# One cast held behind a copy in the forgetting stages, and four stores moved behind eight transpositions: a hybrid attention block

## The chip, the cores and the metric

The kernel runs on one core of a Trainium2 chip. The metric is the device time of one execution in microseconds (us), and lower is better. A core has TensorE (PE, with its weight loads shown apart as PEld), VectorE (DVE), ScalarE (ACT), GpSimd (POOL) and SyncE (SP), which in this kernel issues all DMA transfers. Each engine works through its own instruction queue in order; semaphores order the engines among each other.

## What is computed

The reference is one decoder block with two attention branches over 16 meta tokens and 512 real ones. Cut to what matters here:

```python
u = rmsnorm(h, pre_norm_g)
cq, ckv, k_pe_raw, z_mla, fq, fk, fv, f_logit, z_fox, gate_a, gate_b = split(u @ w_in)
# latent branch, 16 heads: low-rank q, k, v, and 32 rotary dimensions
q = rmsnorm(cq) @ w_uq ; kv = rmsnorm(ckv) @ w_ukv
q_m = concat(q_nope, rope(q_pe)) ; k_m = concat(k_nope, rope(k_pe_raw) for all heads)
y_mla = (causal_attention(q_m, k_m, v_mla) * silu(z_mla)) @ w_br_mla
# forgetting branch, 16 heads: logits get cum[t] - cum[s]
cum = cumsum(log_sigmoid(f_logit + fox_forget_b))
y_fox = (causal_attention(fq, fk, fv, cum) * silu(z_fox)) @ w_br_fox
mixed = (sigmoid(gate_a) * y_mla + sigmoid(gate_b) * y_fox) @ w_out
h = h + rmsnorm(mixed, post_norm_g)
```

All is float32 with a width of 1024.

## The kernel before

Every large product is computed from a high and a low part of each operand: of three products two use the weights' high part, one the low part. Weights come in units of 128 output columns: SP loads the raw weights (`wraw`, 512 KB, three buffers), ACT casts them to the high part (`wh`, line 127, three buffers), POOL subtracts to get the low part (`wl`, line 102), and then PE works. The raw buffer is free again when POOL is done, `wh` when PE is done with the unit. Loads are asked for three units ahead.

The attention runs in 16 stages, one for each pair of heads of each branch, in turn: even stages are forgetting ones (`br` = 1), odd ones latent (`br` = 0). `si` is the stage, from 0; `pr` the pair. A stage is, on PE:

- scores of the first three query blocks (`s0`: blocks of 144, 272 and 400 columns), then the values of the stage before (`va`, line 801, tile `ov`), then the scores of the fourth block (`s1`);
- the list `fill`: projections that this and the next stage need. A forgetting stage fills with the forgetting z unit (8 steps), the next latent q (2 steps), the latent z (its first step is `fill[11]`), latent k and v. A latent stage fills with the next forgetting q, the first half of k, v, and the second half of k. A step's first call casts the weights of its unit.

In between, at places set by hand, come `n0` and `n1` (line 767): they scale the exponentials to probabilities in two float16 parts (`pn`) and issue eight DMA transpositions (`pt`), which the values of that stage need, in the next one. `fill[0]` issues the transposition of the stage's value vectors (`vp`).

The copies of projected K and Q out of PSUM (`hlk`, `hlq`, line 239 on ACT, then DVE for the low part) are recorded in `halved`, one entry for each half of K. The exponentials are line 763, DVE's score reductions line 755.

Rotary queries of the latent branch are computed for eight heads at a time (`pe_unit`). Those of the first two heads go to their place (`QP`) directly; those of the other six of the first group are stored to DRAM by `store0(x, 2, 8)`, two stores for each of two x, 192 KB each (`qpe_dram<-gT`), and read back one pair at a time, 256 KB with both halves, by `load_qp` (`QP<-qpe_dram`), for the first time for stage 3. The second group, all eight heads, is stored in stages 6 and 7 behind `n1`.

PE's order is the order in the program. The other queues are ordered by a planner that works with its own estimates of when things are ready. Two means bind it: `tc.issue_after(x)` puts what is traced in its block behind x on x's engine, without a wait for x to end; `keep_in_program_order` puts an instruction behind the one that was traced before it on its engine. Casts are issued behind `behind[0]` while that list has an entry:

```python
with tc.issue_after(behind[0]) if behind else nullcontext():
    nc.scalar.copy(wh[:, :n], raw[:, :n])
```

and every DMA that is traced while `written[0]` is true is kept in program order on SP.

Of the kernel before, what the change touches and what calls it, by code (L numbers as in the profile page):

```python
# [54 lines left out]
def block_kernel(ctx: ExitStack, tc: tile.TileContext, x, meta_tokens, pre_norm_g, w_in, fox_forget_b,  # L55
# [28 lines left out]
    written, sums_out = [False], []  # L84
    behind, through, first_t, exps, halved = [], [], [], [], {}
# [126 lines left out]
    def run(steps):  # L212
        for _, fn in steps:
            fn()
# [309 lines left out]
    def gate_unit():  # L524

        i, br = gates.pop(0)

        def done(_, ps):
            ths[i, br] = thp.tile([128, S], F32, tag="th", name=f"th{i}{br}")
            nc.scalar.activation(ths[i, br], ps, AF.Tanh, scale=0.5)  # L530
        return unit(f"pg{i}{br}", win_w((O_GA, O_GB)[br], i), u_act, KD, REAL, done)


    with ExitStack() as att:
# [289 lines left out]
        def feed(br, pr):  # L824

            q = (q_mla, q_fox)[br](pr)
            k = (k_mla, k_fox)[br](pr)
            v, vts[br, pr] = v_unit(br, pr)
            return q, k, v
# [7 lines left out]
        pe, rest0, store0 = pe_unit(0)  # L837
# [5 lines left out]
        for si, (br, pr) in enumerate(stages):  # L843
            last = si + 1 == len(stages)
            if not last:
                q, k, v = feed(*stages[si + 1])
            if br == 1:

                za, zb = z_unit(1, pr), z_unit(0, pr)
                fill = (vts[br, pr] if pr else begun) + za + q + zb[:4] + k + zb[4:6] + v + zb[6:]  # L850
            elif not last:

                fill = vts[br, pr] + q + k[:KD] + v + k[KD:]
            else:
                g = gate_unit()
                fill = vts[br, pr] + g + gate_unit() + gate_unit()
# [9 lines left out]
        for si, (br, pr) in enumerate(stages):  # L866
            s0, s1, n0, n1, va = attention(br, pr)

            for fn in [s0] + late + [s1]:
                fn()  # L870

            fill = fills[si]
            if si == 0:

                run(fill[:5])
                run(vts[1, 0] + pe_rest)
                n0()
                n1()
                first_t.extend(through)
                run(fill[5:])  # L880
            else:
                run(fill[:1])
                if si == 1:

                    written[0] = True
                    for x in range(2):
                        store0(x, 2, 8)
                    written[0] = False
                run(fill[1:5])
                if si == 1:  # L890

                    behind[:] = exps[:1]
                if si == 2:
                    behind.clear()
                n0()
                run(fill[5:12])
                n1()
                if 6 <= si < 8:

                    written[0] = True  # L900
                    rest1(si - 6)
                    written[0] = False
                run(fill[12:])
            written[0] = False
            if si == 1:

                behind[:] = [halved[("k", 1, 1), 0]]
            late = [va]
# [146 lines left out]
```

## Time and profile before

| | us |
|---|---|
| median of 3 runs | 625.7 |
| lowest and highest | 625.54, 627.62 |
| span of the profiled execution, first to last instruction | 622.1 |
| PE busy in it | 599.9 (96%) |
| ACT busy | 330.8 (53%) |
| DVE busy | 315.4 (51%) |
| POOL busy | 265.5 (43%) |

Of the profiled execution only the span is on record; what lies around it is taken as the difference to the median, 3.6 us. PE's busy time is of pipelined matmuls whose ends are modelled, so PE can be late where it is counted as busy. Times of single events below are counted from the start of the span. Stage 0 has its first scores at about 66.8 us, stage 15 its last at about 401; behind the stages come the gates, the branch outputs and the output projection, which PE runs through without a break.

### The profile page before, as it was taken

What the parts mean: (1) busy time and instruction counts of PE and PEld (TensorE: products, weight loads), DVE (VectorE), ACT (ScalarE), POOL (GpSimd) and SP (SyncE); (2) the same over time, 40 slices, a digit from 0 to 9 for tenths busy, and PEclk for the clock granted to TensorE, in tenths of its full rate; (3) what the DMA queues carried; (4) which work ended last, traced back from release to release, by engine and by line L of the source; (5) the groups of instructions that cost most, each with busy time, mean ns of one, the idle gap of its engine ahead of it and who ended that gap; (6) DMA issues with size and microseconds to landing.
All of it is one profiled execution on the core that took longest, in us unless ns stands there. A gap on an engine that the chain in (4) does not pass through costs nothing.

```text
span 622.1 us, 11008 instructions
## 1 busy us (share of the span) xinstructions
PE 599.9 (96%) x3811; PEld 507.3 (82%) x3811; DVE 315.4 (51%) x922; ACT 330.8 (53%) x757; POOL 265.5 (43%) x270
## 2 busy tenths in 40 slices
PE   5997999799999999999999999999999999999996
PEld 5886789689889789888888898887888888888885
DVE  3848647555765764674675657627321122024034
ACT  7755745655764864774676657656322222232321
POOL 4307535352346543344443523542744444444610
PEclk9999999899999999999999999999999999999999
DMA  9422589969798787878579697871433332333602
GB/s 289 99 76 53 120 178 142 242 141 190 145 186 161 149 208 154 172 167 204 140 161 174 145 169 159 187 168 40 136 102 101 102 93 79 100 103 115 257 34 102
DMA packets 223512, 89.31 MB, mean 144 GB/s; under 512 B 141708, under 2 KB 216852, under 8 KB 223456
## 3 DMA queue, kind: packets, MB, share of 16 engines
q1 hardware_dynamic: 223456, 88.61, 61.9%
q8 instruction: 30, 0.49, 0.3%
q14 instruction: 26, 0.21, 0.1%
HBM read 54.43 MB, written 4.00 MB: 94 GB/s over the span
## 4 chain that ended last, share of the span: by engine, by line
PE 86%; DVE 5%; ACT 4%; issue 2%; DMA 1%; SPq 0%; POOL 0%; DVEq 0%; ACTq 0%
PE z L96 14%; PE pg L96 14%; PE py L96 14%; PE v L96 9%; PE fq L96 7%; PE po L96 7%; PE fk L96 7%; PE st L96 5%; PE ov L96 3%; PE psm L96 3%; DVE sf L755 2%; PE mq L96 2%; ACT wh L127 2%; PE mk L96 1%; DVE vh L690 1%
## 5 line engine op out<-in xcount | busy, mean ns | idle before, releaser
L102 POOL TENSOR_TENSOR wl<-wraw,wh 128x1024 fp32r<-128x1024 f32 (+1 forms) x90 | 207.3, 2308 | 221.0 <-ACT wh L127 219.2
L127 ACT CAST wh<-wraw 128x1024 fp32r<-128x1024 f32 (+1 forms) x90 | 89.9, 1003 | 172.3 <-issue 47.7
L763 ACT ACTIVATE sf<-sf,nb 128x144 f32<-128x144 f32 (+3 forms) x128 | 72.0, 564 | 15.8 <-DVE nb L755 15.8
L791 DVE SCALAR_TENSOR_TENSOR pn<-sf,ri,pn 128x128 f16<-128x128 f32 (+3 forms) x128 | 68.8, 576 | 13.1 <-ACT pn L790 12.2
L790 ACT ACTIVATE pn<-sf,ri 128x128 f16<-128x128 f32 (+3 forms) x128 | 61.5, 551 | 19.9 <-ACT sf L763 17.9
L938 DVE SCALAR_TENSOR_TENSOR tb<-th,py 128x512 f32<-128x512 f32 x16 | 11.0, 687 | 101.9 <-PE py L96 101.9
L96 PE MATMUL st<-hlk,hlq 64*128 64x272 f32 (+3 forms) x480 | 52.8, 317 | 5.0 <-ACT hlk L239 4.1
L96 PE MATMUL z<-uTh,wh 128*128 128x512 f32 x128 | 50.8, 397 | 0.0
L96 PE MATMUL pg<-uTh,wh 128*128 128x512 f32 x128 | 50.2, 392 | 0.0
L96 PE MATMUL z<-uTh,wl 128*128 128x512 f32 x128 | 50.1, 391 | 0.0
L96 PE MATMUL z<-uTl,wh 128*128 128x512 f32 x128 | 49.9, 390 | 0.0
L96 PE MATMUL pg<-uTh,wl 128*128 128x512 f32 x128 | 49.8, 389 | 0.0
L96 PE MATMUL pg<-uTl,wh 128*128 128x512 f32 x128 | 49.8, 389 | 0.0
L96 PE MATMUL py<-gh,wh 128*128 128x512 f32 x128 | 49.8, 389 | 0.0
L96 PE MATMUL py<-gl,wh 128*128 128x512 f32 x128 | 49.8, 389 | 0.0
L96 PE MATMUL py<-gh,wl 128*128 128x512 f32 x128 | 49.8, 389 | 0.0
L96 PEld LDWEIGHTS st<-hlk,hlq 64*128 64x128 f32 x480 | 37.0, 186 | 15.0 <-ACT hlk L239 5.8
L755 DVE CUSTOM_DVE_ANT_0 sf<-st,maskt 128x272 f32<-128x272 f32 (+2 forms) x128 | 48.4, 434 | 0.9 <-PE st L96 0.8
L777 POOL TENSOR_TENSOR mt<-sf,ri 128x96 f32<-128x96 f32 (+1 forms) x32 | 9.5, 297 | 89.4 <-DVE ri L772 66.5
L96 PE MATMUL v<-uTh,wh 128*128 128x256 f32 (+1 forms) x128 | 36.6, 286 | 2.3 <-DVE hlk L102 2.3
L96 PE MATMUL v<-uTl,wh 128*128 128x256 f32 (+1 forms) x128 | 36.5, 285 | 0.0
L96 PE MATMUL fk<-uTl,wh 128*128 128x256 f32 (+1 forms) x128 | 36.4, 285 | 0.0
(189 smaller groups left out, 1403.3 us busy)
## 6 DMA issues: line engine op xcount, KB each, us to landing
wraw<-in_w_in_dram SPq DMA_DIRECT2D x56, 512.0 KB
wraw<-in_w_br_fox_dram SPq DMA_DIRECT2D x8, 512.0 KB
wraw<-in_w_br_mla_dram SPq DMA_DIRECT2D x8, 512.0 KB
wraw<-in_w_out_dram SPq DMA_DIRECT2D x8, 512.0 KB
pt<-pn SPq DMA_TRANSPOSE x128
xr<-in_x_dram SPq DMA_DIRECT2D x4, 512.0 KB
out_dram<-yo SPq DMA_DIRECT2D x8, 256.0 KB
QP<-qpe_dram SPq DMA_DIRECT2D x7, 256.0 KB
```

The lines of the kernel that those rows point to most:

```text
L96: nc.tensor.matmul(*a, **k)
L102: eng.tensor_tensor(out=lo, in0=src, in1=f32(hi), op=ALU.subtract)
L127: nc.scalar.copy(wh[:, :n], raw[:, :n])
L690: nc.vector.scalar_tensor_tensor(out=lo, in0=p, scalar=sc[:, 3:4], in1=hi, op0=ALU.mult, op1=ALU.subtract)
L755: nc.vector.tensor_tensor_reduce(out=sf_of(h, b)[:, c0 : c0 + w], in0=ps[h][:, o : o + w], in1=maskt[:, m0 : m0 + w], scale=-scale, scalar ...
L763: exps[g] = nc.scalar.activation(sf, sf, AF.Exp, bias=sums["nb"][:, h, b : b + 1], scale=-1.0, accum_out=sums["su"][:, h, b : b + 1]).ins
L777: nc.gpsimd.tensor_tensor(out=mt, in0=src, in1=ri.unsqueeze(3).broadcast_to([128, 2, nb_, META]), op=ALU.mult)
L790: nc.scalar.activation(hi, sf, AF.Copy, scale=rib)
L791: nc.vector.scalar_tensor_tensor(out=lo, in0=sf, scalar=rib, in1=hi, op0=ALU.mult, op1=ALU.subtract)
L938: nc.vector.scalar_tensor_tensor(out=tb[br], in0=ths[i, br], scalar=1.0, in1=py, op0=ALU.add, op1=ALU.mult)
```

## The change

Two edits in the stage loop, for all stages but the first.

1. In forgetting stages (`br` = 1, from stage 2 on), the list `behind` holds the copy of the second half of this stage's K while `fill[11]` runs, so that the cast of the first latent z unit's weights is issued behind that copy on ACT. In stage 2 such a hold already stands for an earlier cast, that of the forgetting z unit, behind the copy of the first half.
2. In stage 1, the four stores of the rotary queries of heads 2 to 7 are traced behind `n1` instead of behind `fill[0]`. As they are kept in program order, they stand on SP behind the last of that stage's eight transpositions, and no longer behind the transposition of the value vectors.

```diff
             else:
                 run(fill[:1])
+                run(fill[1:5])
+                if si == 1:
+                    behind[:] = exps[:1]
+                if si == 2:
+                    behind.clear()
+                n0()
+                run(fill[5:11])
+                if br:
+                    behind[:] = [halved[("k", 1, pr), 1]]
+                run(fill[11:12])
+                if br:
+                    behind.clear()
+                n1()
                 if si == 1:
                     written[0] = True
                     for x in range(2):
                         store0(x, 2, 8)
                     written[0] = False
-                run(fill[1:5])
-                if si == 1:
-                    behind[:] = exps[:1]
-                if si == 2:
-                    behind.clear()
-                n0()
-                run(fill[5:12])
-                n1()
                 if 6 <= si < 8:
```

No instruction is added or removed.

More of the change, by code (lines that the diff above doesn't have):

```diff
@@ L882, in block_kernel @@
                 run(fill[:1])
-                if si == 1:
[L885 to L888, printed above, removed]
                 run(fill[1:5])
@@ L895, in block_kernel @@
                 n0()
-                run(fill[5:12])
-                n1()
+                run(fill[5:11])
[4 more added lines that the diff above has]
+                    behind.clear()
+                n1()
+                if si == 1:
+                    written[0] = True
+                    for x in range(2):
+                        store0(x, 2, 8)
+                    written[0] = False
                 if 6 <= si < 8:
```

## The prediction

> **What bounds the kernel now.** I read the page first, for the chain that ended last, then that chain in order of time, then each engine around the two places where the chain leaves PE, then SP's queue.
>
> ```profile
> span 622.1 us, 11008 instructions
> PE 86%; DVE 5%; ACT 4%; issue 2%; DMA 1%; SPq 0%; POOL 0%; DVEq 0%; ACTq 0%
> ```
>
> PE carries the chain, so time can only be won where PE stands still. The chain, in order of time (start, length, what):
>
> ```profile
> 109.63 4.28 DMA wraw<-in_w_in_dram
> 113.99 1.04 ACT wh L127
> ...
> 116.97 2.93 PE ov L96 x26
> ...
> 121.07 5.66 PE z L96 x24
> ...
> 158.46 1.05 ACT wh L127
> ...
> 164.06 5.68 PE z L96 x24
> ...
> 375.78 1.05 ACT wh L127
> ```
>
> Twice a pattern shows. In stage 2 (the second forgetting stage) the chain runs through a weight load, then a cast of weights on ACT. In the six later forgetting stages (first 158.46, last 375.78) a cast of 1.05 us stands in the chain just ahead of the scores. The cast is that of the first latent z unit: it takes the buffer that the K unit frees with its last matmul, and the copy of the second half of K waits for the same matmul. Around it in stage 4, all engines in order of time:
>
> ```profile
> 159.39 0.30 PE L96 MATMUL st<-CT,ONE 64*128 64x272 f32 x2
> 159.41 0.36 ACT L239 CAST hlk<-fk 128x256 fp32r<-128x256 f32 x1
> 159.83 0.30 PEld L96 LDWEIGHTS st<-hlk,hlq 64*128 64x128 f32 x4 [0.36 <-ACT hlk L239]
> 160.15 0.30 DVE L755 CUSTOM_DVE_ANT_0 sf<-st,maskt 128x144 f32<-128x144 f32 x1
> 160.49 0.42 ACT L763 ACTIVATE sf<-sf,nb 128x144 f32<-128x144 f32 x1 [0.71 <-DVE nb L755]
> 160.85 2.04 PE L96 MATMUL ov<-pt,vp 80*64 80x512 f16 x26
> ```
>
> The 1.05 us is not PE's loss. Scores of the first two query blocks need only the first half of K and run until 159.69; only the 400-column block waits for the copy. The same place in a latent stage, where nothing waits, gives the price (PE alone):
>
> ```profile
> 179.17 0.29 PE L96 MATMUL st<-KPL,QP 64*128 64x272 f32 x2
> ...
> 179.84 0.34 PE L96 MATMUL st<-KPH,QP 64*128 64x400 f32 x2
> 180.02 0.35 PE L96 MATMUL st<-KPL,QP 64*128 64x400 f32 x2
> 180.29 0.41 PE L96 MATMUL ov<-pt,vp 80*64 80x512 f16 x2
> ```
>
> From the last 272-column pair to the values' first matmul it takes 1.12 us with five sets of 400 columns; one set is 0.18, so four take 0.94. The forgetting stage takes 160.85 - 159.39 = 1.46. It loses 0.52.
>
> **The cast order, stages 4 to 14.** The change issues that cast behind the copy. The copy then starts when the cast did, 158.46, and ends at 158.82; the cast ends at 159.87. The loss of 0.52 goes: 6 x 0.52 = 3.1 us. The lower bound is the wait that the row names, 0.36, so 2.2. What is late next? DVE's first reduction can start when PE's block ends, 159.69 instead of 160.15, so the first exponential comes 0.46 earlier, at 160.03, still after the cast's 159.87. The transpositions of the probabilities follow the exponentials and move with them, so their lead before the next stage's values stays nearly what it was. The cast's remainder on POOL ends 0.4 later; who waits for that is a rival below.
>
> **Stage 2: cast order and stores together.** PE alone:
>
> ```profile
> 111.74 0.30 PE L96 MATMUL st<-CT,ONE 64*128 64x272 f32 x2
> 115.36 1.28 PE L96 MATMUL st<-hlk,hlq 64*128 64x400 f32 x6 [3.31 <-ACT hlk L239]
> ```
>
> By starts, from the last 272-column pair to z: 121.07 - 111.74 = 9.33 us here, 164.06 - 159.39 = 4.67 in stage 4, and there 0.52 is lost as well. So 9.33 - 4.67 + 0.52 = 5.2 us are lost in stage 2. Not all of it is idle time. Behind the gap PE runs at half speed for a while (stretches of the span; the last three columns are the granted clock, the DMA engines' busy share and GB/s):
>
> ```profile
> 94.00:98.00 4.00, 4.00 (x20) 3.26 (x19) 3.95 (x8) 3.81 (x8) 3.74 (x6) 1.00 0.39 120
> 115.30:117.00 1.70, 1.64 (x10) 1.14 (x12) 1.60 (x9) 0.99 (x6) 1.70 (x1) 0.55 1.07 265
> ```
>
> The first row is for the stores: DMA engines busy 0.39, 120 GB/s, while SP is past them. SP's queue around stage 1, and around stage 7, where two stores of the second group already stand behind the transpositions; between them the start of the values in stage 9 on PE stands last:
>
> ```profile
> 91.63 4.07 SPq L90 DMA_DIRECT2D qpe_dram<-gT  x4
> ...
> 110.33 3.74 SPq L90 DMA_TRANSPOSE pt<-pn  x2
> ...
> 121.19 1.18 SPq L90 DMA_TRANSPOSE pt<-pn  x1
> ...
> 124.71 8.58 SPq L90 DMA_TRANSPOSE pt<-pn  x6
> ...
> 231.80 10.65 SPq L90 DMA_TRANSPOSE pt<-pn  x8
> 242.50 1.24 SPq L90 DMA_DIRECT2D qpe_dram<-gT  x2
> ...
> 249.76 0.35 SPq L90 DMA_DIRECT2D QP<-qpe_dram  x1
> ...
> 257.57 9.38 SPq L90 DMA_TRANSPOSE pt<-pn  x6
> ```
> ```profile
> 268.63 0.41 PE L96 MATMUL ov<-pt,vp 80*64 80x512 f16 x2
> ```
>
> The cast order by itself would win little in stage 2. The values there need all eight transpositions of stage 1, the last of which SP issued until 110.33 + 3.74 = 114.07. The shortest way from the end of such an issue to the values is in stage 8: 268.63 - (257.57 + 9.38) = 1.68. So the values, now at 116.97, could not start before 115.75.
>
> Moving the stores gives the rest. Four issues (4.07 us on SP) leave the place ahead of every load and transposition of stage 1. The last transposition then ends at 110.0 or sooner; without the stores' data in front, the last two would take 2 x 1.33 (10.65 for eight in stage 7) and not 3.74, so 108.9 to 110.0. Add 1.68: 110.6 to 111.7. PE's values are due at 111.74 + 0.94 = 112.68, so they don't wait. The z unit's weights (issued 109.63, landed 4.28 later) come by 105.6 + 4.28 = 109.9. The cast's turn is later: it starts 0.93 ahead of the 272-column row in stage 4, here at 110.8, and 0.36 of copy come before it, 111.2. Stage 2 gains its whole 5.2; if the transpositions came no earlier at all, 1.2 by the values' bound above.
>
> **Where the moved stores cost.** Behind the last transposition stand the stores, then whatever SP issues next: weight loads, the next values' transposition, the reload of QP for stage 3, and the eight transpositions of stage 2. The reload reads what the stores write, so SP stands still at it until they have landed. Two rows show that this happens:
>
> ```profile
> SPq L90 <- DMA qpe_dram<-gT: 4.3, 1, 4.3
> ```
> ```profile
> qpe_dram<-gT SPq DMA_DIRECT2D x4, 256.0 KB
> qpe_dram<-gT SPq DMA_DIRECT2D x4, 192.0 KB
> ```
>
> In stage 7, two stores of 256 KB held the reload for 249.76 - 242.50 = 7.3 us after the first issue. Here it is four of 192 KB. At the 120 GB/s of the row above, the extra 256 KB take 2.1 us: 9.4. Doubling the whole wait gives 14.5. I take 10.0, near the low end, because part of the 7.3 is the transposition ahead.
>
> So the reload is free at 109.4 + 10.0 = 119.4, the first transposition of stage 2 goes at 119.9, the eight take 12.1 (121.19 to 133.29), and 1.68 later, at 133.6, the values of stage 3 may start. They are due 180.29 - 160.85 = 19.4 after those of stage 2: 132.1. I charge 1.5 us. The ends: nothing (reload placed behind the transpositions, or landed sooner), and 5.6 to 6.7 with 14.5 us.
>
> By the Trainium skill (DMA: Bandwidth & Descriptors, "Why a DMA increments its semaphore by 16 and not by 1", the part on how many engines) a DMA uses the largest number up to 16 that divides the slowest dimension of both sides. Six heads would give six engines, and 6/16 = 0.375 agrees with the 0.39; eight heads would give eight, and estimated by that page four stores take 3.2 us longer than two rather than 2.1: the charge would be about 2 us and the time 619.4. It speaks against the change: the stores are slow wherever they stand.
>
> The sum, against the profiled execution (span 622.1; the median of 625.7 lies 3.6 above it, and I keep that difference): -3.1 - 5.2 + 1.5 = -6.8, a span of 615.3 and a time of **618.9 us**.
>
> For the charge in stage 3 I count idle time alone. By rows, a gap of 3.31 was followed by a clock of 0.55; if a gap of 1.5 were followed by a shorter such stretch in proportion, 0.9 us would be added. By the Trainium skill (TensorE: Matmul & The Clock Gate, "What's actually happening") the clock halves after an idle window of about 3.4 us, and by that rule 1.5 us of idle adds nothing; the 3.31 with the 0.55 behind it agrees roughly.
>
> **Rivals.** *The reload never binds* (it is placed late, or the stores land in under 9 us): 617.4. For it, SP has work to issue meanwhile; against it, the one row of 4.3 us is just this wait. Chance 0.27, the forecast 0.40.
>
> *The reload takes back stage 2* (14.5 us): 617.4 + 5.6 to 6.7 = 623.0 to 624.1, no measurable change against half a per cent of 625.7, which is 3.1 us and about what can be told here. For it: two stores alone stopped SP for 4.3. Against: weight loads, too, stood in that wait. Chance 0.15.
>
> *The held cast goes too late, slower.* If the order puts the cast behind the six exponentials and not right behind the copy, its remainder on POOL frees the raw weights later, and SP's next loads stand ahead of the transpositions:
>
> ```profile
> L763 ACT ACTIVATE sf<-sf,nb 128x144 f32<-128x144 f32 (+3 forms) x128 | 72.0, 564 | 15.8 <-DVE nb L755 15.8
> ```
> ```profile
> 159.59 2.38 POOL L102 TENSOR_TENSOR wl<-wraw,wh 128x1024 fp32r<-128x1024 f32 x1 [1.80 <-ACT wh L127]
> ```
> ```profile
> 161.99 2.46 SPq L90 DMA_DIRECT2D wraw<-in_w_uq_dram  x4
> 165.53 1.18 SPq L90 DMA_TRANSPOSE pt<-pn  x1
> ...
> 169.42 7.99 SPq L90 DMA_TRANSPOSE pt<-pn  x6
> ```
>
> Six times 0.564 is 3.4: POOL ends at 165.4 instead of 161.97, the loads at 167.8, the first transposition is 2.7 later than the 165.1 (165.53 - 0.46) that it would have. The last one's slack is 180.29 - 177.41 - 1.68 = 1.2, so the values lose 1.5 a stage, in seven stages 10.5: 618.9 + 10.5 = 629.4. It turns the whole to slower than now once a stage loses 1.0. Against it: at 158.82 ACT is free and the cast is ready, the exponentials are not for another 1.2. Chance 0.07. Other shifts of the order, either way, 0.11, most of them within 3 us of the forecast.
>
> **How the numbers follow.** Faster by over 0.5%, under 622.6: 0.40 + 0.27, 0.08 of the other shifts and 0.03 of the second rival, 0.78. Within 0.5%: the rest of that rival and 0.02, 0.14. Slower: 0.07 and 0.01, 0.08. The range runs from 617.0 (full gain, with a little for the run) to 623.0 (the beginning of the second rival).
>
> **What would show it.** Right: in every forgetting stage from 2 on, ACT's copy of K's second half before the cast, and no wait of PE's weight loads for it; in stage 2 values about 2 us behind K's last matmul, with the clock at 1.00; SP's stores between stage 1's last transposition and stage 2's first; a PE gap of one to two us before the values of stage 3, and SP waiting some us for the stores to land. Wrong: a gap there over 3 us with a low clock, casts behind exponentials, or values in stage 2 that still wait for transpositions.

## The result: a quarter of the forecast

Medians of 22 executions of each kernel on the same chip: 624.3 us after the change (622.0 to 627.4), 626.9 before (623.4 to 628.0). The ratio over these executions is 0.9972, 95% interval 0.9959 to 0.9985, or 1.75 us less; the two medians themselves lie 2.5 us apart. The forecast was 6.8 less, its range 2.7 to 8.7 less than the median then shown. The sign was right and the size wrong. The gain is within the half per cent that was called the bound of what can be told; over this many executions it can just be told.

The page of the changed kernel, its span and the chain by engine:

```profile
span 621.6 us, 11000 instructions
PE 88%; DVE 4%; ACT 3%; issue 2%; DMA 1%; POOL 0%; SPq 0%; DVEq 0%; ACTq 0%
```

PE has two points more of the chain, and the spans differ by 0.5 only. The chain in order of time (start, length, what) shows where both the gain and the loss are:

```profile
111.13 1.88 PE st L96 x24
113.01 1.97 PE ov L96 x26
...
116.15 5.67 PE z L96 x24
...
134.64 3.17 DMA pt<-pn
...
137.94 3.81 PE ov L96 x22
143.74 5.67 PE fq L96 x24
...
161.08 1.88 PE st L96 x24
162.96 1.97 PE ov L96 x26
```

Stage 2 (the first three rows) has its weight load and its cast out of the chain, and stage 4 (the last two) its cast. In stage 3 a transposition of probabilities stands in the chain that was not there before, and behind it the values take 3.81 us where stage 2 takes 1.97 for the same work.

On ACT in stage 4 the order is the one meant, copy of K, then cast; and PE (the second fence, its last two rows) goes from its last 272-column pair to the values in 162.89 - 161.93 = 0.96 us, where it took 1.46:

```profile
161.11 0.37 ACT L239 CAST hlk<-fk 128x256 fp32r<-128x256 f32 x1 [0.57 <-PE fk L96]
161.38 1.05 ACT L127 CAST wh<-wraw 128x1024 fp32r<-128x1024 f32 x1
```
```profile
136.93 0.60 PE L96 MATMUL ov<-pt,vp 80*64 80x512 f16 x1 [4.49 <-DMA pt<-pn]
137.94 3.81 PE L96 MATMUL ov<-pt,vp 80*64 80x512 f16 x25 [0.41 <-DMA pt<-pn]
...
161.93 0.28 PE L96 MATMUL st<-CT,ONE 64*128 64x272 f32 x2
...
162.89 0.41 PE L96 MATMUL ov<-pt,vp 80*64 80x512 f16 x2
```

The first two of PE's rows are stage 3: PE stands 4.49 us for a transposition, 0.41 for another, and then works slowly. The granted clock (third column from the right) behind that gap, and from 9 us later:

```profile
136.90:140.00 3.10, 2.66 (x13) 1.35 (x15) 0.12 (x1) 2.50 (x6) 1.15 (x4) 0.50 1.08 265
...
146.00:150.00 4.00, 4.00 (x23) 3.42 (x22) 2.42 (x6) 2.62 (x5) 0.81 (x4) 1.00 0.76 149
```

From stage 2's z to stage 3's first query projection it takes 27.6 us where it took 20.1: 7.5 us lost, 4.9 of them idle; the other 2.6 are put down to the low clock. Why the transposition is late is on SP's queue:

```profile
110.48 3.97 SPq L90 DMA_DIRECT2D qpe_dram<-gT  x4
114.56 1.84 SPq L90 DMA_DIRECT2D wraw<-in_w_in_dram  x1
120.31 0.35 SPq L90 DMA_DIRECT2D QP<-qpe_dram  x1
120.75 0.39 SPq L90 DMA_DIRECT2D wraw<-in_w_in_dram  x1
121.23 2.10 SPq L90 DMA_TRANSPOSE vp<-vh  x1
123.38 0.58 SPq L90 DMA_DIRECT2D wraw<-in_w_in_dram  x1
124.06 1.29 SPq L90 DMA_TRANSPOSE pt<-pn  x1
...
127.64 8.27 SPq L90 DMA_TRANSPOSE pt<-pn  x6
```

The reload goes 120.31 - 110.48 = 9.8 us after the first store. Then come two weight loads and the transposition of the value vectors, 3.1 us of issues, and only then, at 124.06, the first transposition of stage 2.

### The profile page after: what moved, and what is told of

It is laid out like the page before. It is cut to its first block, busy times and chain, and to the rows that moved or that the text cites. A ratio compares the mean times of both kernels' runs of the same rounds, so it can differ in the third digit from the quotient of the medians.

```text
span 621.6 us, 11000 instructions
## 1 busy us (share of the span) xinstructions
PE 598.6 (96%) x3811; PEld 509.0 (82%) x3811; DVE 316.1 (51%) x922; ACT 330.5 (53%) x757; POOL 265.2 (43%) x270
## 4 chain that ended last, share of the span: by engine, by line
PE 88%; DVE 4%; ACT 3%; issue 2%; DMA 1%; POOL 0%; SPq 0%; DVEq 0%; ACTq 0%
PE z L96 14%; PE pg L96 14%; PE py L96 14%; PE v L96 9%; PE fk L96 7%; PE fq L96 7%; PE po L96 7%; PE st L96 6%; PE ov L96 4%; PE psm L96 3%; DVE sf L755 2%; PE mq L96 2%; PE mk L96 1%; DVE vh L690 1%; DMA ht<-in_x_dram 1%
## 5 line engine op out<-in xcount | busy, mean ns | idle before, releaser
L96 PE MATMUL st<-hlk,hlq 64*128 64x272 f32 (+3 forms) x480 | 50.8, 311 | 0.7 <-DVE nb L755 0.2
L96 PE MATMUL ov<-pt,vp 128*64 128x512 f16 (+4 forms) x416 | 35.1, 318 | 4.9 <-DMA pt<-pn 4.9
L96 PEld LDWEIGHTS <-vp 128*64 128x64 f16 (+1 forms) x416 | 23.0, 113 | 18.7 <-issue 10.1
```

Of the source, the lines that this page charges most:

```text
L96: nc.tensor.matmul(*a, **k)
```

## The experiments

Theory: SP stands at the reload until the four stores have landed, and stage 3 pays for it. Rivals: the cast order costs something too; the place of the reload or SP's order alone is to blame; the bytes of the stores rather than their shape. Ratios are to the kernel before, with 95% intervals.

### The parts alone

**Cast order alone**, the stores in their old place.

```diff
                 run(fill[:1])
+                if si == 1:            # the four stores
...
                 n1()
-                if si == 1:            # the four stores
```

> The cast order alone, the stores back in their old place. Theory (the two edits act in different places: the cast order gives 0.5 us in each of stages 4 to 14, the stores' move wins stage 2 and loses more in stage 3): 3.0 us from stages 4 to 14, and in stage 2 at most 1.2 more, because the values there still wait for stage 1's last transposition, issued until about 114; stage 3 stays as before, no gap ahead of its values. Time 3 to 4.5 us under before, ratio 0.993 to 0.995, faster than the whole change. Rival (the two edits need each other): under 1.5 us gained.

Measured: 621.7 us, ratio 0.9944 (0.9919 to 0.9969), 0.0028 less than with both edits, though the two intervals overlap. Stages 4 to 14 win 3.05 us. Stage 3 has no gap. Stage 2 waits for its last transposition instead of a cast, and in the profiled execution it even loses 1.2 us (34.6 from stage 1's first scores to stage 2's z, 33.4 before): the gap is nearly as long as the old one, and the low clock behind it lasts longer. That execution took 625.1 us, one of the slowest of the twelve, so its terms (3.05 won, 1.2 lost) give less than the ratio does. Stage 2's values on PE:

```profile
119.03 0.60 PE L96 MATMUL ov<-pt,vp 80*64 80x512 f16 x1 [3.23 <-DMA pt<-pn]
119.97 3.79 PE L96 MATMUL ov<-pt,vp 80*64 80x512 f16 x25 [0.34 <-DMA pt<-pn]
```

**Stores alone**, without the hold on the cast.

```diff
-                if br:
-                    behind[:] = [halved[("k", 1, pr), 1]]
                 run(fill[11:12])
-                if br:
-                    behind.clear()
```

> The stores' move alone, the cast left free. Theory: stage 2 wins about 4.7 us (its weights and transpositions come early; 0.5 for the cast stays lost), stage 3 loses about 7.5 as in the changed kernel; stages 4 to 14 as before. 2.5 to 3.5 us slower than before, ratio 1.004 to 1.0055. Rival (the loss in stage 3 comes from the cast edit or from ACT): no gap ahead of stage 3's values, faster than before by 4 us.

Measured: 627.3 us, 1.0016 (0.9997 to 1.0036), less slow than expected and not told apart from no change. Stage 2 wins 4.65 us, half a microsecond less than in the whole change; the same gap stands in stage 3 (4.26 and 0.42), and stages 4 to 14 are as before. So from stage 4 on the gain is of the cast order, and the loss in stage 3 is of the stores. In stage 2 the parts do not simply add: without the stores' move the cast order wins nothing there.

**No stores at all**: the first group's stores and the reloads of pairs 1 to 3 are left out, for a bound; heads 2 to 7 then use the rotary queries of the first pair.

```diff
-            dma(f32(QP), qpe_dram[2 * pr : 2 * pr + 2]...)
+            pr < 4 or dma(f32(QP), qpe_dram[2 * pr : 2 * pr + 2]...)
...
-                        store0(x, 2, 8)
+                        pass
```

> The whole change without the four stores and without the reloads of QP for pairs 1 to 3: the latent scores of heads 2 to 7 then use the rotary queries of the first pair. This is the bound of what any place or form of the stores can win. Theory: stage 2 gains its 5.2, stage 3 loses nothing, stages 4 to 14 gain 3.0: 8 us under before, ratio 0.986 to 0.988, no PE gap over 0.5 us between 90 and 400. Rival (stage 3's gap has another cause beside the stores, such as the earlier weight loads): a gap ahead of stage 3's values remains.

Measured: 617.2 us, 0.9853 (0.9829 to 0.9877). SP issues the first transposition of stage 2 at 119.30, the stage-3 values run in 2.04 us, and no gap over 0.16 us is left on PE between 90 and 400. So all of stage 3's loss is of the stores and the reload. Stage 3's values on PE, and the issue of stage 2's value vectors' transposition on SP, which is needed below:

```profile
133.88 2.04 PE L96 MATMUL ov<-pt,vp 80*64 80x512 f16 x26
```
```profile
112.98 3.87 SPq L90 DMA_TRANSPOSE vp<-vh  x1
```

### The reload, or the stores?

**The reload later**, behind the sixth transposition of stage 2.

```diff
-            dma(f32(QP), ...)
+            with tc.issue_after(through[0]) if pr == 1 else nullcontext():
+                dma(f32(QP), ...)
```

> The whole change, with the reload of QP for stage 3 issued behind the sixth of stage 2's eight transpositions; nothing else on SP changes place. Theory (SP stands at the reload until the stores land, and two weight loads, the values' transposition and eight transpositions stand behind it): the first transposition of stage 2 is issued at 118 to 119 instead of 124.1, the values of stage 3 start at 132 to 133 instead of 136.9, with no low clock behind; 6 to 8 us under the changed kernel, ratio to before 0.986 to 0.989. Rival (the stores' own transfer fills the DMA queue, and what is issued behind them lands late wherever the reload stands): first transposition early on SP, but long issues, the last one's end still at 134 or later; within 2 us of the changed kernel.

Measured: 622.9 us, 0.9951 (0.9931 to 0.9972); the expected gain was missed. SP never stands for the reload now, yet the first transposition goes at 122.42, only 1.6 us earlier than in the change (124.06), because the issues themselves fill the time: 4.00 us for the four stores, 3.12 for two weight loads (1.17 without stores), 4.31 for the value vectors' transposition. The last is hardly of the stores: this issue took 4.29 us before the change and 3.87 without any store, and only in the change, behind the long wait, 2.10. And the reload now lands too late for stage 3's scores:

```profile
117.33 4.31 SPq L90 DMA_TRANSPOSE vp<-vh  x1
...
131.25 0.58 SPq L90 DMA_DIRECT2D QP<-qpe_dram  x1
```
```profile
134.36 0.49 PE L96 MATMUL st<-KPH,QP 64*128 64x144 f32 x2 [3.92 <-DMA QP<-qpe_dram]
```

My theory was too narrow: take the wait at the reload away, and SP needs most of that time for its issues.

**A third of the bytes**: heads 2 and 3 in stage 1, heads 4 to 7 in stage 3.

```diff
-                if si == 1:
+                if si in (1, 3):
                     for x in range(2):
-                        store0(x, 2, 8)
+                        store0(x, *((2, 4) if si == 1 else (4, 8)))
```

(The reload for stage 5 is held behind a transposition, as above.)

> In stage 1 only heads 2 and 3 are stored, four stores of 64 KB instead of 192 KB; heads 4 to 7 follow in stage 3 behind its transpositions, with their reload held behind the sixth transposition of stage 4. To be read in stage 2: how long the reload for stage 3 waits. By the bytes, a third of them should take a third of the 8 us that follow the first landing: reload about 5 us after the first store instead of 9.8, stage 3's values 3 to 5 us earlier than in the changed kernel. By the Trainium skill (DMA: Bandwidth & Descriptors, Why a DMA increments its semaphore by 16 and not by 1) two heads would run on two engines, as much for each engine as before, and the reload would wait 9 to 10 us as before.

Measured, one execution: 627.1 us. Four stores of 64 KB instead of 192 KB hold the reload for 120.90 - 112.57 = 8.3 us, against 9.8, and counted from the end of the fourth issue 5.7 against 5.9: the time hardly depends on the bytes.

```profile
112.57 2.59 SPq L90 DMA_DIRECT2D qpe_dram<-gT  x4
...
120.90 0.35 SPq L90 DMA_DIRECT2D QP<-qpe_dram  x1
```

**One head to a store**, two heads in each of stages 1, 3 and 5, eight stores of 32 KB each time. Heads 6 and 7 are stored after their buffer has been loaded anew, so their scores use other numbers.

```diff
-                if si == 1:
+                if si in (1, 3, 5):
                     for x in range(2):
-                        store0(x, 2, 8)
+                        store0(x, si + 1, si + 3, 1)   # one head to a store
```

> The whole change, with the stores cut by head: heads 2 and 3 in stage 1, 4 and 5 in stage 3, 6 and 7 in stage 5, each as eight stores of 32 KB (16 rows each) behind that stage's transpositions. More issues on SP (eight of about 0.6 us against four of 0.7 to 1.6), the same rows to each reload. Theory (what holds stage 2's transpositions back is that the stores' transfer takes 8 us in the DMA queue, and the reload, the loads and the transpositions stand behind it): with each store over all engines the transfer is over 2 to 3 us after the last issue, the first transposition of stage 2 goes at about 118, stage 3's values start within 1 us of 132.5, the clock stays at 1.00 there; 5.5 to 8 us under the changed kernel, ratio to before 0.986 to 0.989. Rival (SP's queue itself is full: eight issues more or less cost as much as the wait): values of stage 3 at 135 or later, within 3 us of the changed kernel.

Measured: 626.2 us, 1.0003 (0.9985 to 1.0021). The reload now goes 117.53 - 112.32 = 5.2 us after the first store, nearly all of it SP's own issues (the eight stores 3.82, two weight loads 1.01), and up to stage 3's query projection this kernel is 4.1 us ahead of the change. It gives that back and more from stage 4 on, where the later stores make new gaps (1.74 us at 202, 1.44 and 1.01 at 271 to 274).

```profile
112.32 3.82 SPq L90 DMA_DIRECT2D qpe_dram<-gT  x8
...
117.53 0.83 SPq L90 DMA_DIRECT2D QP<-qpe_dram  x1
```

### SP's queue, or the engines that carry the data?

The four stores, in the same place of the program, issued by GpSimd on its own queue, then by ScalarE on its own. The reload stays on SP.

```diff
-                    dma(qpe_dram[8 * g + a : 8 * g + b, i, x], rr[x][16 * a : 16 * b, i])
+                    dma(qpe_dram[8 * g + a : 8 * g + b, i, x], rr[x][16 * a : 16 * b, i],
+                        None if g else nc.gpsimd.dma_start)      # or nc.scalar.dma_start
```

> The changed kernel with its four stores issued by GpSimd on a queue of its own, in the same place of the program (behind stage 1's second group of weights, so about 7 us earlier in time, since SP's queue no longer holds them); the reload stays on SP, behind the last transposition of stage 1. Theory (what stage 3 lost was SP's queue standing behind 4.0 us of store issues and a transfer that held every later load and transposition of that queue for 10 us): the reload goes by 115, the first transposition of stage 2 by 119, no gap over 0.6 us ahead of stage 3's values, no low clock behind it, 6 to 8 us less than the kernel before, ratio 0.987 to 0.990. Rival (the stores hold the transfer engines themselves, from whatever queue they come): stage 1's last transposition lands behind 117 instead of 113, the values of stage 2 wait 2 to 3 us with a low clock behind, ratio 0.993 to 0.997.

> The same with the four stores issued by ScalarE on its queue, among stage 1's casts. Theory: SP's queue is as free as with GpSimd's, but four issues of 0.7 to 1.6 us stand ahead of the casts of the second factor of the rotation of stage 2 on ScalarE (about 4 us), and PE waits for them at most 1 to 2 us there; stage 3 as with GpSimd; ratio 0.988 to 0.992. Rival (transfer engines held): as for GpSimd's, 0.993 to 0.998.

Measured: GpSimd 626.2 us, 1.0003 (0.9983 to 1.0023); ScalarE 625.1 us, 0.9977 (0.9958 to 0.9996). The theory of SP's queue fell. GpSimd issues the first store at 102.69, 7.8 us ahead of SP in the change; SP's queue has no store in it, and its transpositions are held all the same, 6.79 us for two issues that took 3.74 before the change; PE then waits 4.37 us in stage 2. Stage 3 loses nothing any more (20.1 us from z to the query projection), but from stage 1's first scores to stage 2's z it takes 35.1 us, 28.2 in the change: the loss has moved with the stores. The groups of transfers (name, queue, count, size, median us from issue to landing), SP in order of time, and PE:

```profile
qpe_dram<-gT POOLq DMA_DIRECT2D x4, 192.0 KB, 8.7
```
```profile
108.75 6.79 SPq L90 DMA_TRANSPOSE pt<-pn  x2
```
```profile
116.96 4.45 PE L96 MATMUL ov<-pt,vp 80*64 80x512 f16 x26 [4.37 <-DMA pt<-pn]
```

A store of 192 KB lands 8.7 us after its issue (the first row's last column), from a queue of its own. ScalarE is worse off in another way than expected: its last two issues take 7.7 us together, and the copies of K and the casts stand behind them; PE waits 4.19 us behind the copy of K's first half instead of 1 to 2. ScalarE's queue in that run:

```profile
104.40 7.70 ACTq L90 DMA_DIRECT2D qpe_dram<-gT  x2
```

**The stores' shape.** The DRAM layout is turned from heads first to parts first, so that a store writes one block of 96 rows, not six of 16. Bytes, place and queue stay; the second group's stores and all seven reloads change with the layout.

```diff
-    qpe_dram = dram.tile([NH, 2, 2, 16, S], ...)
+    qpe_dram = dram.tile([2, 2, NH, 16, S], ...)
...
-            dma(f32(QP), qpe_dram[2 * pr : 2 * pr + 2].rearrange("h i x f s -> (h i x f) s"))
+            for h in range(2):
+                dma(f32(QP[64 * h : 64 * h + 64]), qpe_dram[:, :, 2 * pr + h].rearrange("i x f s -> (i x) f s"))
...
-                    dma(qpe_dram[8 * g + a : 8 * g + b, i, x], rr[x][16 * a : 16 * b, i])
+                    dma(qpe_dram[i, x, 8 * g + a : 8 * g + b].rearrange("h f s -> (h f) s"), rr[x][16 * a : 16 * b, i])
```

> The changed kernel with the rotary queries laid out in DRAM by part first and head second, so that each of the four stores writes one contiguous block of 96 rows where it wrote six blocks of 16; the reload of a pair becomes two loads of 64 rows, one for each head (in all seven stages that reload), and SP's order shifts by one load in places. Same bytes, same place, same queue. Theory (six engines were held for 10 us by a store that used six of sixteen): the semaphore climbs by 16 steps, the four stores land within 4 to 6 us of the first issue instead of 9.8, the reload goes at 116 instead of 120.3, the first transposition of stage 2 lands by 125 instead of 129.2, the gap ahead of stage 3's values is under 1 us with no low clock behind it: 4 to 6 us less than the change as it is, ratio to the kernel before 0.987 to 0.991. Rival (the bytes, or the issues on SP, are what holds): stores land after 9 to 10 us as before, ratio 0.996 to 0.999. Second rival (the reloads by head use few engines and hold the transpositions of every latent stage): stage 3 is won but stages 5 to 13 lose 0.5 to 1 us each, ratio 0.993 to 0.998.

Measured: 621.6 us, 0.9930 (0.9906 to 0.9954), by 2.6 us (0.9972 to 0.9930) better than the change, and short of what was expected. The four issues take 2.05 us instead of 3.97, and the reload goes 5.1 us after the first:

```profile
110.05 2.05 SPq L90 DMA_DIRECT2D qpe_dram<-gT  x4
...
115.12 1.30 SPq L90 DMA_DIRECT2D QP<-qpe_dram  x2
...
116.98 4.65 SPq L90 DMA_TRANSPOSE vp<-vh  x1
...
122.37 1.26 SPq L90 DMA_TRANSPOSE pt<-pn  x1
```

So the shape of the stores is shown as the cause of the 10 us for which the reload waits: same bytes, same queue, half the time. By the Trainium skill (DMA: Bandwidth & Descriptors, "Why a DMA increments its semaphore by 16 and not by 1") the slowest dimension of both sides sets how many engines carry a transfer: six for the old store, two for the 64 KB one, sixteen for the new and for a single head. 192 KB on six and 64 KB on two are 32 KB an engine, and 9.8 and 8.3 us agree with that. What the width doesn't buy back is in the last two rows: the value vectors' transposition takes 4.65 us to issue, more than the 2.10 in the change and about what it took before (4.29) and without stores (3.87). So the first transposition comes only 1.7 us earlier than in the change. Gaps of 2.24 and 1.45 us are left in stage 3, and from stage 2's z to stage 3's query projection it still takes 26.5 us, against 27.6 in the change and 20.1 before. Whether the reload, now two loads of 64 rows in four blocks, adds to that is not shown. The second rival did not show: from stage 3's query projection to stage 14's z it is 237.1 us, and 237.2 in the change.

### Towards a better kernel

**A hold in the latent stages.** In the chain of the kernel with the cast order alone, latent stages such as stage 7 go through a cast on ACT ahead of the scores of the fourth block (the second group), like the one which the change removed. Here the cast of the value unit's weights (in stage 15, of the third gate unit's) is held behind the latent gate's activation in stages 3, 7, 9, 11, 13 and 15.

```diff
-                run(fill[12:])
+                run(fill[12:17])
+                if not br and si > 1 and si != 5:
+                    behind[:] = [halved["z", 0, pr]]       # the gate's activation
+                run(fill[17:18])
+                if not br and si > 1 and si != 5:
+                    behind.clear()
+                run(fill[18:])
```

On the kernel with one-head stores, then on the cast order alone, then with the stores by GpSimd, then with the wide stores:

> The cut stores, and the same kind of hold in the latent stages 3, 7, 9, 11, 13 and 15: the cast of the V unit (in stage 15 of the third gate unit) behind the activation of the latent z unit, which waits for the same matmul. In the kernel before, the second part of the scores takes 1.86 there and 1.43 in stages 1 and 5. Theory: 0.4 us in each of six stages, 2.4 to 2.6 us under the kernel with the cut stores alone; ratio to before 0.982 to 0.985. Rival (those scores wait for DVE's other work, not for the cast): no gain, within 0.5 us.

> The cast order alone (stores in their old place) with one hold more: in stages 3, 7, 9, 11, 13 and 15 the cast of the values' weights is held behind the latent branch's gate activation, as the run with one-head stores had it. If the two add up: 0.9944 less 0.45 x 6 = 2.7 us of 626.8 (0.0043, of which the earlier run showed 0.0025), so 0.990 to 0.992. If the latent hold only pays where the stages before it were shifted by the one-head stores: 0.994 to 0.996.

> Stores by GpSimd and the latent hold together: the product of the two parts. By the theory 0.983 to 0.987; by the rival of the transfer engines 0.990 to 0.993.

> The same with the latent hold of the runs before. If they add: 0.0045 less than without the hold, 0.983 to 0.987, and faster than the cast order with the hold alone (0.9898). By the first rival 0.991 to 0.995.

Measured: 624.7 us, 0.9978 (0.9960 to 0.9996); 620.1 us, 0.9898 (0.9876 to 0.9919); 622.6 us, 0.9938 (0.9915 to 0.9962); 621.4 us, 0.9916 (0.9891 to 0.9942). Against the same kernels without the hold that is 0.0025, 0.0046, 0.0065 and 0.0014 less; in the first and the last pair the intervals overlap, and the sums expected for the last two (0.983 to 0.987) did not come. The traces say it more closely: with the cast order alone, from a stage's first scores to its query projection, it is 6.12 us without the hold and 5.68 with it in each of the six stages (stage 15: to its gate projection), 2.6 us together, or 0.0042. The scores of the second group in stage 7, before (cast order alone) and with the hold, from the chain:

```profile
231.43 0.49 DVE sf L755
...
231.97 0.86 PE st L96 x9
```
```profile
228.38 1.42 PE st L96 x20
```

In the first the chain is on DVE and ACT before these scores, in the second it stays on PE.

**The stores in stage 0**, behind its transpositions, with the hold; wide and narrow.

```diff
                 first_t.extend(through)
+                for x in range(2):
+                    store0(x, 2, 8)
...
-                if si == 1:            # the four stores
```

> The kernel of the wide stores with the latent hold, its four stores moved one stage earlier, behind the transpositions of stage 0, where the trace shows SP without work for about 5 us and stage 0's values 2.5 us behind their last transposition. Theory (five microseconds of sixteen engines fit there; the reload then never waits for a store): the stores land by 92 us, stage 1's first transposition is late by at most 1 us, the reload of stage 1 goes by 111, no gap over 0.6 us ahead of the values of stages 1, 2 and 3; 2 to 4 us less than the wide stores in stage 1, ratio 0.983 to 0.988. Rival (the stores push the weights of stage 1's first units, which are loaded behind them): a gap of 1 to 3 us in stage 0 or 1 takes it back, ratio 0.989 to 0.993.

> The same place in stage 0 and the same hold with the stores as they were, six blocks of 16 rows each. If six engines for 10 us are the cost wherever they stand, stage 1's values transposition and first score transposition land 4 to 6 us late and stage 1 or 2 shows a gap of 1 to 4 us: ratio 0.989 to 0.995. If the place is what counts: as the wide ones, 0.983 to 0.988.

Measured: wide 616.2 us, 0.9853 (0.9815 to 0.9891), the fastest kernel here that does all the work; narrow 621.9 us, 0.9920 (0.9897 to 0.9943). Width counts, as the two intervals here lie apart; so does the place (0.9916 in stage 1 with wide stores and the hold), though there the intervals just touch. SP with the wide stores, then with the narrow ones:

```profile
85.61 1.99 SPq L90 DMA_DIRECT2D qpe_dram<-gT  x4
...
95.46 2.48 SPq L90 DMA_TRANSPOSE pt<-pn  x2
```
```profile
87.98 3.99 SPq L90 DMA_DIRECT2D qpe_dram<-gT  x4
...
103.22 1.18 SPq L90 DMA_TRANSPOSE pt<-pn  x1
```

From the first store to stage 1's first transposition it is 9.9 us with wide stores and 15.2 with narrow ones, whose stage 1 then has gaps of 1.42 and 2.70 us. With the wide stores the reload goes at 110.23, and the values of stage 3 start without a wait, a little stretched; stage 3 takes its 20.1 us again. PE's row, and the chain of that kernel by engine:

```profile
132.19 2.44 PE L96 MATMUL ov<-pt,vp 80*64 80x512 f16 x26
```
```profile
PE 94%; ACT 2%; DVE 2%; DMA 1%; issue 0%; POOL 0%; SPq 0%; DVEq 0%; ACTq 0%
```

DVE, ACT and issue are nearly out of the chain. This profiled execution is the quickest of its kernel's six (614.0 us, clock 0.998), so the medians are what to compare.

## Why the prediction was wrong

- **Cast order, stages 4 to 14: right.** 3.1 forecast; in the trace 0.50 a stage, 2.99 from stage 3's query projection to the end of stage 15; the run of that edit alone 3.05.
- **Stage 2: right.** 5.2 forecast. From the first scores of stage 1 to stage 2's z it takes 28.20 us instead of 33.38, 5.18 less. "By itself the cast order would win little" held too: in that run PE waited 3.23 us for a transposition, and stage 2 won nothing.
- **Stage 3: the step that failed.** 1.5 forecast, 7.5 measured. The wait of the reload was right in size (10.0 forecast, 9.8 measured, from a first store 1.1 us later than the 109.4 assumed), but partly by luck: it was scaled by bytes at 120 GB/s, and with a third of the bytes the wait was still 8.3. What failed is the next clause, "the first transposition of stage 2 goes at 119.9", half a microsecond behind the reload. It went 3.75 us behind it, at 124.06, since two weight loads and the value vectors' transposition stand between. The prediction names these issues, but ahead of the reload, where their time would have fallen into the wait. The profile of before had it. Behind the reload at 249.76 the first transposition went at 253.86, 4.1 us later, and in stage 2 itself 7.0 us later:

```profile
114.17 0.53 SPq L90 DMA_DIRECT2D QP<-qpe_dram  x1
...
115.89 4.29 SPq L90 DMA_TRANSPOSE vp<-vh  x1
120.29 0.52 SPq L90 DMA_DIRECT2D wraw<-in_w_in_dram  x1
121.19 1.18 SPq L90 DMA_TRANSPOSE pt<-pn  x1
```

In both places the prediction's view of SP's queue leaves out what stands in between. I took the order on SP from the change's text and did not write it out.

- **The clock, a second part of that step.** I counted idle time alone. A gap of 1.5 us might have cost nothing more; one of 4.9 was followed by a clock of 0.50, which cost 2.6. So 3.4 of the 6.0 us missed are idle time, 2.6 the clock.
- **The median.** I carried 3.6 us from span to time; the new executions have 623.4 - 621.6 = 1.8. The other 1.8 came in because the profiled execution of before was quicker than its median. The terms by the traces (-3.0, -5.2, +7.5) make -0.7, the spans -0.5, the ratio -1.75 and the medians -2.5; executions of one kernel differ by more than that.
- **The rivals.** "The reload takes back stage 2" had the mechanism with a bound of 14.5 us for the wait; it came true in size by another route, with 9.8 of wait and 4 behind it. The held cast was never late.

That the stores are slow wherever they stand was noted in the prediction, priced there at 0.5 us more, and left out of the sum. Followed further it would have asked what else uses those engines.

Not settled: the 1.0 us by which the ratio shows more than the sum of the terms. Behind a gap of about the same length the low clock lasted 3.7 us in the profile of before (115.3 to 119.0) and 5 us in that of the cast order alone, so executions can differ there, but no run shows that this is it. Nor was it tried to load the queries back in one block together with the wide stores.

## What to carry to other kernels

When a transfer is moved in a queue, write out every issue between it and the next thing that PE needs, with its wait; a step "then the next one goes" is a term of the sum too. A slow store delays other transfers, from whatever queue it is issued: look at its shape (how many blocks of the slowest dimension) and at its place. Here the shape alone left 6.4 of the 7.5 us that stage 3 lost; shape and place together left none. Where a gap grows beyond 2 us, price the slow work behind it as well.

## What the runs showed of the hardware

- Store time follows the blocks, not the bytes: four stores of 192 KB in six blocks held the reload for 9.8 us, 64 KB in two blocks for 8.3, 192 KB in one run of 96 rows for 5.1. Behind eight of 32 KB it went after 5.2, most of which was issues.
- A queue of its own does not free the others: two transpositions on SP took 6.79 us to issue beside GpSimd's stores, 3.74 before the change. On ScalarE two issues took 7.7 us, and for all but the first 0.6 of that none of its other work ran.
- Idle windows shorter than I had from the row of 3.31 were followed by about half clock: 2.90 us (wide stores with the hold), then 0.59; 2.70 (narrow stores in stage 0), then 0.57; and 2.18 (cast order with the hold, in stage 2), then 0.50 for 3 us. By the Trainium skill (TensorE: Matmul & The Clock Gate, "What's actually happening") the window is about 3.4 us; these three are shorter than that. The granted clock in the stretches behind the first two gaps:

```profile
138.60:141.90 3.30, 3.08 (x26) 2.14 (x24) 0.36 (x2) 2.50 (x6) 1.16 (x4) 0.59 1.15 276
```
```profile
114.00:117.00 3.00, 3.00 (x18) 3.00 (x17) 0.35 (x1) 0.52 (x1) 0.68 (x1) 0.57 0.60 118
```
